# A hybrid decoder block: Conformer merge and part of the output projection as seven-product blocks, with aligned operands

## The chip, the cores and the metric

The kernel runs on one core of one Trainium2 chip. The metric is the device time of one execution in microseconds; the median of several runs is compared. Before the change it is 906.48 us (3 runs, 906.36 to 908.56).

## The reference

One block of a decoder over 512 tokens and 1,024 channels in float32. A norm, one wide projection, three token mixers (dilated attention, a Conformer convolution, a short convolution), a sigmoid gate for each mixer, a merge, an output projection with residual, then a gated MLP with a convolution and a last norm.

```
h = rms_norm(x, norm1_g)
u = h @ w_in
q, k, v, conf_a, conf_gate, sc_b, sc_c, sc_x, gates = split(u)
attn  = dilated_window_attention(...) @ w_attn_out      # 256 -> 1024
conf  = silu(layer_norm(dwconv31(conf_a * sigmoid(conf_gate)))) @ w_conf_out   # 768 -> 1024
short = (sc_b * dwconv3(sc_c * sc_x)) @ w_sc_out         # 768 -> 1024
g = sigmoid(gates)                                       # 3 x 1024 channels
mixed = g[0] * attn + g[1] * conf + g[2] * short
x = x + mixed @ w_o                                      # 1024 -> 1024
up = dwconv3(rms_norm(x, norm2_g) @ w_up)
return rms_norm(x + (silu(f_gate) * f_val) @ w_down, final_g)
```

## The kernel before, in words

Activations are kept transposed: 128 channels on the partitions, 512 tokens along the free axis. A tile is one such 128x512 block in float32. Every operand of a product is split into a high and a low part (names ending in h and l, whi and wlo for weights); a product is hi·hi + hi·lo + lo·hi, three matmuls that add up in one PSUM bank.

**Weights.** The host packs all weights into steps of eight 128x128 units, 128x1024 floats each, in the order in which they are used. For each step SP starts a DMA into one of four buffers (tiles w, r or s), ACT casts the high part (whi, L258), and the low part is either a DVE subtraction (wlo, L263) or, where by_dma says so, ACT writes minus the high part into wlo (L260) and POOL starts a DMA that adds the step's weights to it in SBUF (L261). This preparation runs AHEAD = 3 steps ahead of the matmuls, with four buffers each for whi and wlo.

**Quads.** The gates' projection, and most of w_up, are done as quads (function quad): a 2x2 block of output (two channel groups, two token halves of 256) by seven products instead of eight. The seven weight operands are, in this order, r11, s1, s2, r12, s3, s4, r22. Three of them are loaded quarters of the block. s1 = r21 + r22 is loaded by SP and added to by a POOL DMA, in one of two extra buffers; s2, s3, s4 are made from the others by DVE subtractions of whole steps (L224). The activation operands are b11, b21, b22 (halves of the tiles) and four sums t1 to t4, made by x_sums: for each of the quad's row pairs, four 256-wide subtractions on DVE, two casts of 512 on ACT, two subtractions for the low parts on DVE. A product has K/2 · 2 · 3 matmuls of 256 columns: 24 for K = 8 row blocks. A quad uses the PSUM banks a, b and c. Banks b and c (kinds qb and qc) have one buffer each, so a quad's second product, which opens bank c, waits until the previous quad's bank c has been read.

**Around the change.** The gates for one mixer and four output groups are one quad (gt01 is row half 0 of mixer 1, the Conformer). Its four results go through a sigmoid on ACT (tiles sg, L920). Then merge multiplies the mixer's own output projection (tile mo) by sg and adds it to mixed (tile mx). For the Conformer this is four output tiles of 18 matmuls with 512 columns for each half (K = 6), after which mixed is split into mx..h and mx..l. The order is gt02, gt12, the attention's gt00 and merge, gt10 and merge, gt01, merge, gt11, merge. The output projection follows: eight tiles wo of 24 matmuls with 512 columns, residual and split for the second norm (xh) behind each. w_up follows.

**What sets the order.** Each engine's instructions are put in order at build time by a scheduler that works from the program's order; side work is put in a queue and taken from it at slots, each piece behind an anchor instruction. Engines run in order, so an instruction that waits holds up all that stand behind it on that engine.

Of the kernel before, what the change touches and what calls it, by code (L numbers as in the profile page):

```python
# [53 lines left out]
FW = SW + KC * 3  # L54
NPAR = FW + 2 * KF * 3


# [3 lines left out]

def quad_units(name, pairs):

    return [(name, 2 * i + odd, p[f]) for f, odd in ((0, 0), (0, 1), (1, 0), (1, 1)) for p in pairs for i in range(KD // 2)]


def plan():

    steps = [("n", c) for c in range(54)]
    c = 54  # L70
    for name, _, n in BRANCHES:
        for q in range(2):
# [12 lines left out]

def weight_units():

    aw = CONF // P
    a0, g0 = 18, 18 + aw
    b0, c0, x0 = 30, 36, 42  # L90
    gate0 = 48
    u = []
    for js in ((0, 1), (2,), (3,), (4,), (5,)):
        for k in range(KD):
            u += [("w_in", k, m + j) for j in js for m in (a0, g0)]
    for g in range(3):
        for m in (0, 6):
            for p in range(2):
                u += [("w_in", k, m + 2 * g + p) for k in range(KD)]
        if g < 2:  # L100
            for k in range(KD):
                u += [("w_in", k, (12, 14)[g] + p) for p in range((2, 4)[g])]
    for j in range(KC):
        for m in (c0, x0, b0):
            u += [("w_in", k, m + j) for k in range(KD)]
    u += [("w_sc_out", k, j) for j in range(KD) for k in range(KC)]
    for name, br, n in BRANCHES:
        for q in range(2):
            c = gate0 + br * KD + 4 * q
            u += quad_units("w_in", [(c, c + 1), (c + 2, c + 3)])  # L110
            u += [(name, k, 4 * q + i) for i in range(4) for k in range(n)] if name != "w_sc_out" else []
    for j in range(KD):
        u += [("w_o", k, j) for k in range(KD)]
# [44 lines left out]
def trunk(ctx: ExitStack, tc: tile.TileContext, xT, wts, par, bias, sel, ident, fg, out):  # L158
    nc = tc.nc
    cp = ctx.enter_context(tc.tile_pool(name="cp", bufs=1))  # L160
    wp = ctx.enter_context(tc.tile_pool(name="wp", bufs=3))
    tp = ctx.enter_context(tc.tile_pool(name="tp", bufs=49))
    early = ctx.enter_context(ExitStack())
    ap = ctx.enter_context(tc.tile_pool(name="ap", bufs=KC))
    sp = ctx.enter_context(tc.tile_pool(name="sp", bufs=2))
    kp = ctx.enter_context(tc.tile_pool(name="kp", bufs=8))
    psum = ctx.enter_context(ExitStack())
# [40 lines left out]
    def w_source(c):  # L208
# [8 lines left out]
        def quarter(n):  # L217
            t = w_tile(c, n)
            nc.sync.dma_start(t, wts[i + ("r11", "r12", "r21", "r22").index(n)])
            quarters[i, n] = t  # L220
            return t

        q = lambda n: quarters[i, n]
        sub = lambda o, a, b: V.tensor_tensor(out=o, in0=a, in1=b, op=ALU.subtract)  # L224
        if kind in ("r11", "r12"):
            t = quarter(kind)
        elif kind == "s1":
            t = quarters[i, "s"] = late["s"].tile([P, UNIT * P], F32, tag="s", name=f"s_{c}")
            nc.sync.dma_start(t, wts[i + 2])
            nc.gpsimd.dma_start(t, wts[i + 3], accum_op=ALU.add)  # L230
        elif kind == "s2":
# [24 lines left out]
    def w_split(c, s):  # L256
        hi, lo = (q[:, s] for q in w_parts(c))
        A.copy(hi, w32s[c][:, s])  # L258
        if by_dma(c):
            anchor[0] = A.activation(lo, hi.bitcast(F32), AF.Copy, scale=-1.0).ins  # L260
            nc.gpsimd.dma_start(lo, wts[steps[c][1]], accum_op=ALU.add)  # L261
            return
# [8 lines left out]
    def ahead(c):  # L271

        while state["prepped"] <= min(c + AHEAD, len(steps) - 1):
            p = state["prepped"]
            w_source(p)
            with ExitStack() as order:
                if p == 4:
                    for q in last:
                        order.enter_context(tc.issue_after(q))
                w_split(p, slice(0, UNIT * P))  # L280
            if p + 1 < len(steps):
# [43 lines left out]

    par_sb = cp.tile([P, NPAR], F32, name="par_sb")

# [16 lines left out]
    ident_sb = cp.tile([P, P], F32, name="ident_sb")  # L344
    sel32 = cp.tile([4, 256], F32, name="sel32")
    sel_sb = cp.tile([4, 256], F32R, name="sel_sb")
# [420 lines left out]

    def x_sums(y, k, parts):
# [3 lines left out]
        hi, lo = (kp.tile([P, 4 * HALF], F32R, tag="kb", name=f"xs{k}{n}") for n in "hl")  # L772
        G = V
        for g in range(2):
# [9 lines left out]
            o = slice(g * S, (g + 1) * S)  # L784
            A.copy(hi[:, o], t)
            G.tensor_tensor(out=lo[:, o], in0=t, in1=hi[:, o].bitcast(F32), op=ALU.subtract)
        for i, n in enumerate(("t1", "t2", "t3", "t4")):
            x[n] = tuple(q[:, i * HALF : (i + 1) * HALF] for q in (hi, lo))
        return x

    def hn_sums(k):
        y = []
        for i in range(2):
            t = t512(name=f"hs{k}{i}")
            hi, lo = hn[2 * k + i]
            tt(t, hi.bitcast(F32), lo.bitcast(F32), ALU.add)
            y.append(t)
        xs[k] = x_sums(y, k, hn)

# [7 lines left out]

    def quad(x, name, done, sum22=None):

        beside = slot_ if sum22 is None else lambda _: side(3)  # L810

        def product(bank, n, fresh=False):
# [5 lines left out]
            for p in range(2):  # L818
                o = bank[:, p * HALF : (p + 1) * HALF]
                for k in range(KD // 2):  # L820
                    b = slice((p * 4 + k) * P, (p * 4 + k + 1) * P)
                    xh, xl = x[k][n]
                    T.matmul(o, hi[:, b], xh, start=fresh and p == k == 0, stop=False, skip_group_check=True)
                    T.matmul(o, hi[:, b], xl, start=False, stop=False, skip_group_check=True)
            for p in range(2):
                o = bank[:, p * HALF : (p + 1) * HALF]
                for k in range(KD // 2):
                    b = slice((p * 4 + k) * P, (p * 4 + k + 1) * P)
                    T.matmul(o, lo[:, b], x[k][n][0], start=False, stop=k == KD // 2 - 1, skip_group_check=True)

# [81 lines left out]

    mixed = [None] * KD

    def gates(q, br):
# [9 lines left out]
    def merge(j, br, g):  # L925
# [47 lines left out]
    x1 = []  # L973
    for j in range(KD):
        ps = ps512(f"wo{j}")
        tile_mm(ps, mixed, j == 0)
        tt(xr[j], ps, xr[j], ALU.add)
        x1.append(xr[j])
        xg2.append(split(xr[j], f"xh{j}", pc(G2 + j)))
        q = t512(name=f"s2{j}")  # L980
        A.activation(q, xr[j], AF.Square)
        sq2.append(q)
        if j == 1:
            acc2 = t512(name="acc2")
            tt(acc2, sq2[0], sq2[1], ALU.add)
        elif j > 1:
            tt(acc2, acc2, q, ALU.add)

# [179 lines left out]
    for t in range(4):  # L1168
        pieces = [(0, slice(0, S))] + ([(1, slice(0, S))] if t < 3 else [(1, slice(0, HALF)), (1, slice(HALF, S))])
        sums = []  # L1170
        for n, (h, cols) in enumerate(pieces):
            for k in range(KF - KEEP, KF):
                down(k, t, (h,), cols)
            if n == len(pieces) - 1:
                bm = most(t, sums)
            sums.append(residual(t, h, cols, n))
        finish(t, bm, sums[-1])
# [53 lines left out]
```

## Time and profile before

| | before |
|---|---|
| median of 3 runs | 906.48 us (906.36 to 908.56) |
| the profiled execution | 907.52 us |
| its span, first to last instruction | 905.7 us |
| mean granted TensorE clock | 0.998 |
| PE busy | 894.3 us, 99% |
| weight load (PEld) busy | 795.7 us, 88% |
| DVE busy | 669.4 us, 74% |
| ACT busy | 533.1 us, 59% |
| POOL busy | 92.8 us, 10% |

The profiled execution is some 1 us above the median. Busy time is the time in which an engine has an instruction in work; a matmul's own duration covers its passage through the array, so the matmuls' starts, not their durations, tell how fast PE goes. All times in the views are microseconds from the span's start.

### The profile page before, as it was taken

To read this page: it belongs to the slowest core of one execution; us is meant where nothing else is said; L and a number is where in the kernel's file an instruction comes from. 1 tells how busy PE (TensorE), PEld (TensorE's weight loads), DVE (VectorE), ACT (ScalarE), POOL (GpSimd) and SP (SyncE) were. 2 spreads that over 40 slices of the span, in tenths; PEclk is the share of its full clock that TensorE was granted. 3 is DMA by queue.
4 is the path that set the end of the run, shared out by engine and by line. 5 is a ranking of instruction groups with operands and counts; after the bars stand their busy time and mean duration, and the time that the engine had idled before them with its cause. 6 is when DMAs were issued, how large, how long until landed. Compare 5 with 4: busy or idle time off the path is not lost.

```text
span 905.7 us, 13395 instructions
## 1 busy us (share of the span) xinstructions
PE 894.3 (99%) x5208; PEld 795.7 (88%) x5208; DVE 669.4 (74%) x943; ACT 533.1 (59%) x823; POOL 92.8 (10%) x118
## 2 busy tenths in 40 slices
PE   9999999999999999999999999999999999999996
PEld 7888989888887879999989888889999999888885
DVE  6679969947999868976575545896898889952225
ACT  7655566656656769744544356766766777831214
POOL 3011112211111100000000011100000000000002
PEclk9999999999999999999999999999999999999999
DMA  8688776776797746666636568855666764443202
GB/s 314 191 196 200 181 181 140 167 169 157 181 212 169 161 92 163 189 161 186 187 84 194 188 159 188 190 114 146 179 165 164 182 168 121 154 131 107 93 1 93
DMA packets 42984, 145.32 MB, mean 160 GB/s; under 512 B 4900, under 2 KB 5416, under 8 KB 42920
## 3 DMA queue, kind: packets, MB, share of 16 engines
q1 hardware_dynamic: 30248, 98.84, 32.3%
q0 software_dynamic: 12384, 45.09, 29.9%
q8 instruction: 41, 0.67, 0.3%
q10 hardware_dynamic: 288, 0.52, 0.2%
q14 instruction: 23, 0.19, 0.1%
HBM read 142.34 MB, written 2.10 MB: 159 GB/s over the span
## 4 chain that ended last, share of the span: by engine, by line
PE 91%; ACT 3%; DMA 2%; DVE 2%; issue 1%; SPq 0%; POOL 0%; ACTq 0%; POOLq 0%
PE dn L1121 4%; PE dn L1119 4%; PE dn L1120 4%; PE mo L310 3%; PE mo L311 3%; PE mo L313 3%; PE up L310 2%; PE up L311 2%; PE up L313 2%; DMA wlo<-wts 2%; PE wo L311 1%; PE wo L313 1%; PE wo L310 1%; PE pv L606 1%; PE pv L605 1%; PE pv L604 1%
## 5 line engine op out<-in xcount | busy, mean ns | idle before, releaser
L258 ACT CAST whi<-w 128x1024 fp32r<-128x1024 f32 (+2 forms) x109 | 110.2, 1011 | 161.3 <-PE dn L1120 66.0
L506 DVE SCALAR_TENSOR_TENSOR cc<-ca,par_sb,cc 128x512 f32<-128x512 f32 x180 | 124.2, 743 | 0.2
L263 DVE TENSOR_TENSOR wlo<-w,whi 128x1024 fp32r<-128x1024 f32 (+2 forms) x51 | 57.0, 1117 | 75.3 <-ACT whi L258 74.7
L261 POOL DMA_DIRECT2D wlo<-wts x72 | 62.8, 872 | 431.3 <-ACT wlo L260 351.1
L258 ACT CAST whi<-r 128x1024 fp32r<-128x1024 f32 x70 | 72.9, 1049 | 48.4 <-PE mo L311 10.3
L260 ACT ACTIVATE wlo<-whi 128x1024 fp32r<-128x1024 f32 x72 | 76.3, 1059 | 16.0 <-PE px L313 4.0
L263 DVE TENSOR_TENSOR wlo<-r,whi 128x1024 fp32r<-128x1024 f32 x56 | 68.2, 1219 | 10.5 <-ACT whi L258 7.9
L1033 DVE SCALAR_TENSOR_TENSOR uc<-uu,par_sb,uc 128x511 f32<-128x511 f32 (+1 forms) x72 | 52.0, 746 | 12.4 <-ACT uc L1028 11.9
L263 DVE TENSOR_TENSOR wlo<-s,whi 128x1024 fp32r<-128x1024 f32 x28 | 34.1, 1219 | 9.1 <-ACT whi L258 4.9
L258 ACT CAST whi<-s 128x1024 fp32r<-128x1024 f32 x28 | 29.3, 1046 | 18.2 <-DVE s L224 13.4
L230 POOL DMA_DIRECT2D s<-wts x14 | 12.8, 916 | 223.5 <-DMA s<-wts 53.3
L646 ACT ACTIVATE sc<-sc,nm 128x256 f32<-128x256 f32 (+1 forms) x32 | 15.6, 489 | 17.9 <-DVE nm L644 17.9
L1028 ACT ACTIVATE uc<-uu,par_sb 128x512 f32<-128x512 f32 x36 | 25.2, 728 | 0.3 <-DVE uu L363 0.3
L1119 PE MATMUL dn<-whi,fb 128*128 128x512 f32 x64 | 24.9, 389 | 0.0
L1120 PE MATMUL dn<-whi,fb 128*128 128x512 f32 x64 | 24.9, 389 | 0.0
L1121 PE MATMUL dn<-wlo,fb 128*128 128x512 f32 x64 | 24.9, 389 | 0.0
L1147 POOL TENSOR_TENSOR x1t<-x1t,fg 128x512 f32<-128x512 f32 x4 | 5.6, 1392 | 140.5 <-ACT jk L1129 140.5
L363 DVE TENSOR_TENSOR xr<-wo,xr 128x512 f32<-128x512 f32 x8 | 5.5, 692 | 18.6 <-PE wo L313 16.4
L363 DVE TENSOR_TENSOR sg<-mo,sg 128x512 f32<-128x512 f32 x16 | 11.0, 687 | 10.4 <-PE mo L313 10.2
L224 DVE TENSOR_TENSOR r<-r,r 128x1024 f32<-128x1024 f32 x14 | 17.1, 1224 | 0.4
L224 DVE TENSOR_TENSOR s<-s,r 128x1024 f32<-128x1024 f32 x14 | 17.1, 1222 | 0.3
L224 DVE TENSOR_TENSOR r<-r,s 128x1024 f32<-128x1024 f32 x14 | 17.1, 1218 | 0.0
(3027 smaller groups left out, 3208.7 us busy)
## 6 DMA issues: line engine op xcount, KB each, us to landing
w<-wts SPq DMA_DIRECT2D x100, 512.0 KB, 3.6
wlo<-wts POOLq DMA_DIRECT2D x72, 512.0 KB, 5.8
r<-wts SPq DMA_DIRECT2D x56, 512.0 KB, 4.3
s<-wts SPq DMA_DIRECT2D x14, 512.0 KB, 4.4
s<-wts POOLq DMA_DIRECT2D x14, 512.0 KB, 8.0
xr<-xT SPq DMA_DIRECT2D x8, 256.0 KB, 5.5
xT<-xT SPq DMA_DIRECT2D x7, 256.0 KB, 5.5
w<-wts SPq DMA_DIRECT2D x7, 256.0 KB, 5.5
```

The source lines that it names most:

```text
L258: A.copy(hi, w32s[c][:, s])
L260: anchor[0] = A.activation(lo, hi.bitcast(F32), AF.Copy, scale=-1.0).ins
L261: nc.gpsimd.dma_start(lo, wts[steps[c][1]], accum_op=ALU.add)
L263: anchor[0] = V.tensor_tensor(out=lo, in0=w32s[c][:, s], in1=hi.bitcast(F32), op=ALU.subtract).ins
L310: T.matmul(ps, w[k][0], x[k][0], start=k == 0, stop=False)
L311: T.matmul(ps, w[k][0], x[k][1], start=False, stop=False)
L313: T.matmul(ps, w[k][1], x[k][0], start=False, stop=k == n)
L506: return lambda: V.scalar_tensor_tensor(out=cacc[j], in0=apad[j][:, t : t + 512], scalar=pc(CW + j * CONF_K + t), in1=cacc[j], op0=ALU.mul ...
L1033: V.scalar_tensor_tensor(out=c[:, d:], in0=u[:, : 512 - d], scalar=pc(w + t), in1=c[:, d:], op0=ALU.mult, op1=ALU.add)
L1119: T.matmul(o, fh, wh, start=k == 0, stop=False, skip_group_check=True)
L1120: T.matmul(o, fl, wh, start=False, stop=False, skip_group_check=True)
L1121: T.matmul(o, fh, wl, start=False, stop=k == KF - 1, skip_group_check=True)
```

## The change

The Conformer's merge becomes two quads (merge_quad), one for each half of the output channels, over three pairs of row blocks, K = 6, with weight steps that are 768 wide. Its operand sums are made by conf_sums(k), k = 0 to 2, which are put in the queue when gt01 begins, at a cost of 0.1 each. The output projection does tiles 0 and 1 as before, tiles (2, 3) and (4, 5) as one quad with sums by mx_sums(k), then tiles 6 and 7 as before; tile 0 takes its inputs in the order FIRST. Padding moves all weight and activation tiles to addresses that are multiples of 2,048 bytes (before, nearly all started 96 bytes behind one). The load of s1 is issued two steps earlier in the program. In the tail the last output tile's second half is no longer cut in two, and one multiplication by the final gain goes from POOL to DVE.

```diff
+WO = (0, 1, 6, 7)
+WQ = ((2, 3), (4, 5))
+FIRST = (0, 1, 2, 3, 4, 6, 5, 7)
+PAR_PAD = 608
...
+            if name == "w_conf_out":
+                steps += [(kind, c) for kind in QUAD]
+                NARROW.add(c)
+                c += 4
+                continue
...
+    steps += [("n", c), ("n", c + 1)]
+    steps += [(kind, c + 2) for kind in QUAD]
+    steps += [("n", i) for i in range(c + 6, UP + 2 * PLAIN)]
...
             w_source(p)
+            if steps[p + 3 : p + 4] and steps[p + 3][0] == "s1":
+                w_source(p + 3)
...
-    par_sb = cp.tile([P, NPAR], F32, name="par_sb")
+    par_sb = cp.tile([P, PAR_PAD], F32, name="par_sb")[:, :NPAR]
...
-                for k in range(KD // 2):
-                    b = slice((p * 4 + k) * P, (p * 4 + k + 1) * P)
+                for k in range(len(x)):
+                    b = slice((p * len(x) + k) * P, (p * len(x) + k + 1) * P)
...
+    def mx_sums(k):
+        ms[k] = x_sums(mx32[2 * k : 2 * k + 2], k, mixed)
...
+    def merge_quad(q, g):
+        def done(f, h, src):
+            o = slice(h * HALF, (h + 1) * HALF)
+            for p in range(2):
+                t, m = g[2 * p + f][:, o], mixed[4 * q + 2 * p + f][:, o]
+                tt(t, src[:, p * HALF : (p + 1) * HALF], t, ALU.mult)
+                tt(m, m, t, ALU.add)
+            if f + h == 1:
+                for p in range(2):
+                    j = 4 * q + 2 * p + f
+                    mx32[j] = mixed[j]
+                    mixed[j] = split(mixed[j], f"mx{j}")
+        quad(cq, f"mo{q}", done)
+    def conf_sums(k):
+        cq[k] = sums_of(conf, k, True)
     for name, br, n in BRANCHES:
+        if br == 1:
+            conv.credit = 0.0
+            for k in range(KC // 2):
+                conv.add(lambda k=k: conf_sums(k), 0.1)
         for q in range(2):
             g = gates(q, br)
             slot()
...
+            if br == 1:
+                if q == 1:
+                    for i in range(2):
+                        mx_sums(i)
+                conv.drain()
+                merge_quad(q, g)
+                continue
...
+    for j in WO:
+        ps = ps512(f"wo{j}")
+        tile_mm(ps, [mixed[k] for k in (FIRST if j == 0 else range(KD))], j == 0)
+        if j == 0:
+            for k in range(2, 4):
+                mx_sums(k)
+        tt(xr[j], ps, xr[j], ALU.add)
+        wo_out(j)
+        if j == WO[1]:
...
+            quad(ms, "wo", done, None, lambda _: None)
...
-        nc.gpsimd.tensor_tensor(out=y[0], in0=y[0], in1=fg_sb[0], op=ALU.mult)
...
-        pieces = [(0, slice(0, S))] + ([(1, slice(0, S))] if t < 3 else [(1, slice(0, HALF)), (1, slice(HALF, S))])
+        pieces = [(0, slice(0, S))] + [(1, slice(0, S))]
```

How the change moves instructions is seen best at two engines. First ACT from gt01's copies on (whi are weight casts, sg the sigmoids, which read the banks gt01a, gt01p, gt01c and gt01b; mx0h is the split of mixed). Before:

```order
L841 COPY gt01p_4305<-gt01c_4275 128x512
L258 CAST whi_90_4338<-r22_90_4311 128x1024
L258 CAST whi_91_4370<-w32_91_4342 128x1024
L920 ACTIVATE sg0100_4237<-gt01a_4241 128x256
L920 ACTIVATE sg0110_4239<-gt01a_4241 128x256
L258 CAST whi_92_4403<-w32_92_4374 128x1024
L920 ACTIVATE sg0101_4238<-gt01p_4305 128x256
L920 ACTIVATE sg0111_4240<-gt01p_4305 128x256
L258 CAST whi_93_4435<-w32_93_4407 128x1024
L920 ACTIVATE sg0100_4237<-gt01c_4275 128x256
L920 ACTIVATE sg0110_4239<-gt01c_4275 128x256
```

Now, from the casts of the second operand sums (xs) on:

```order
L818 CAST xs10h_4329<-xt10_4333 128x512
L818 CAST xs11h_4330<-xt11_4338 128x512
L285 CAST whi_93_4490<-s_92_4361 128x768
L285 CAST whi_94_4523<-r12_94_4494 128x768
L818 CAST xs20h_4347<-xt20_4351 128x512
L818 CAST xs21h_4348<-xt21_4356 128x512
L961 ACTIVATE sg0100_4237<-gt01a_4241 128x256
L961 ACTIVATE sg0110_4239<-gt01a_4241 128x256
L961 ACTIVATE sg0101_4238<-gt01p_4305 128x256
L961 ACTIVATE sg0111_4240<-gt01p_4305 128x256
L961 ACTIVATE sg0100_4237<-gt01c_4275 128x256
L961 ACTIVATE sg0110_4239<-gt01c_4275 128x256
```

All eight sigmoids of gt01 stood between weight casts, each pair soon after its bank was done; now they stand in one row behind the last of the six casts xs00h to xs21h.

DVE in the same place of the changed kernel (hs is a tile put together from its parts, xt the sums, L250 a weight subtraction, L290 a weight's low part); all of these rows stand behind gt01c, and behind gt01p:

```order
L817 TENSOR_TENSOR xt11_4338<-hs11_4327,xt10_4333 128x256
L250 TENSOR_TENSOR s_92_4361<-s_92_4361,r11_91_4399 128x768
L819 TENSOR_TENSOR xs11l_4332<-xt11_4338,xs11h_4330 128x512
L392 TENSOR_TENSOR hs20_4343<-cf4h_3438,cf4l_3439 128x512
L392 TENSOR_TENSOR hs21_4345<-cf5h_3518,cf5l_3519 128x512
L812 TENSOR_TENSOR xt20_4351<-hs20_4343 128x256
L290 TENSOR_TENSOR wlo_93_4491<-s_92_4361,whi_93_4490 128x768
L813 TENSOR_TENSOR xt20_4351<-hs21_4345,xt20_4351 128x256
L290 TENSOR_TENSOR wlo_94_4524<-r12_94_4494,whi_94_4523 128x768
L819 TENSOR_TENSOR xs20l_4349<-xt20_4351,xs20h_4347 128x512
L816 TENSOR_TENSOR xt21_4356<-hs21_4345,hs20_4343 128x256
L817 TENSOR_TENSOR xt21_4356<-hs21_4345,xt20_4351 128x256
```

Before, between gt01c and the first merge multiplication DVE had four low parts of weights and gt01p; now these rows of the sums stand there too, and xs21h of ACT's row waits for the second xt21.

DVE at the seam from the Conformer's second quad to the output projection (mx5l and mx7l are inputs of wo0, xs2l and xs3l operand sums of the wo quad, s_115 its s1):

```order
L392 TENSOR_TENSOR mx7_3148<-mx7_3148,sg1111_4734 128x256
L384 TENSOR_TENSOR mx5l_5189<-mx5_3089,mx5h_5188 128x512
L290 TENSOR_TENSOR wlo_115_5214<-s_115_5093,whi_115_5213 128x1024
L384 TENSOR_TENSOR mx7l_5193<-mx7_3148,mx7h_5192 128x512
L250 TENSOR_TENSOR s_115_5093<-s_115_5093,r11_114_5129 128x1024
L250 TENSOR_TENSOR r11_114_5129<-r11_114_5129,r21_118_5317 128x1024
L392 TENSOR_TENSOR xr0_5196<-wo0_5212,xr0_5196 128x512
L290 TENSOR_TENSOR wlo_116_5275<-s_115_5093,whi_116_5274 128x1024
L392 TENSOR_TENSOR xr1_5198<-wo1_5273,xr1_5198 128x512
L812 TENSOR_TENSOR xt20_5244<-mx4_3053 128x256
L816 TENSOR_TENSOR xt21_5249<-mx5_3089,mx4_3053 128x256
L813 TENSOR_TENSOR xt20_5244<-mx5_3089,xt20_5244 128x256
```

Before, mixed was split tile by tile and each wo tile was followed by one low part of weights, one split and one sum of squares. Now a low part of 1,024 stands between mx5l and mx7l, and twelve rows of sums stand behind xr1, which waits for the tile wo1.

## Rows read from the trace of the kernel before

**Rows 1.** The page, part 1: busy time of each engine.
```profile
PE 894.3 (99%) x5208; PEld 795.7 (88%) x5208; DVE 669.4 (74%) x943; ACT 533.1 (59%) x823; POOL 92.8 (10%) x118
```

**Rows 2.** Busy time, granted clock and DMA by stretch (us), for all engines.
```profile
400.00:510.00 110.00, 110.00 (x724) 101.44 (x723) 71.81 (x84) 48.43 (x74) 4.33 (x5) 1.00 0.54 156
510.00:555.00 45.00, 45.00 (x200) 37.19 (x200) 20.58 (x28) 24.75 (x31) 4.10 (x5) 1.00 0.65 175
```

**Rows 3.** PE's waits over the whole span: total us, times, longest.
```profile
PE gt00a L829 <- DMA wlo<-wts: 0.5, 1, 0.5
```

**Rows 4.** The chain of waits, 425 to 560 us: start, us, what.
```profile
432.10 0.96 PE gt01a L829 x8
...
434.98 0.96 PE gt01c L829 x8
...
453.09 1.36 PE mo L313 x6
...
457.17 1.36 PE mo L313 x6
...
512.26 1.81 PE wo L313 x8
517.70 1.81 PE wo L313 x8
```

**Rows 5.** PE in order of time: first matmul of gt01, first of the Conformer's merge.
```profile
430.03 0.28 PE L823 MATMUL gt01a<-hn0h,whi 128*128 128x256 f32 x1
...
450.18 0.40 PE L310 MATMUL mo<-cf0h,whi 128*128 128x512 f32 x1
```

**Rows 6.** DVE in order of time, 307 to 309 us: operand sums of the gate quads.
```profile
307.10 0.69 DVE L363 TENSOR_TENSOR hs<-hn4h,hn4l 128x512 f32<-128x512 f32 x1
307.70 0.68 DVE L363 TENSOR_TENSOR hs<-hn5h,hn5l 128x512 f32<-128x512 f32 x1
308.31 0.42 DVE L778 TENSOR_TENSOR xt<-hs 128x256 f32<-128x256 f32 x1
308.64 0.42 DVE L782 TENSOR_TENSOR xt<-hs,hs 128x256 f32<-128x256 f32 x1
```

**Rows 7.** DVE in order of time, 432 to 452 us: the last gate quad of row half 0.
```profile
433.05 1.22 DVE L224 TENSOR_TENSOR r<-r,s 128x1024 f32<-128x1024 f32 x1
434.19 1.22 DVE L263 TENSOR_TENSOR wlo<-r,whi 128x1024 fp32r<-128x1024 f32 x1
...
438.93 0.70 DVE L363 TENSOR_TENSOR gt01c<-gt01b,gt01p 128x512 f32<-128x512 f32 x1 [1.60 <-PE gt01b L829]
```

**Rows 8.** ACT in order of time, the same stretch.
```profile
441.78 0.65 ACT L920 ACTIVATE sg<-gt01a 128x256 f32<-128x256 f32 x2
...
447.54 0.65 ACT L920 ACTIVATE sg<-gt01c 128x256 f32<-128x256 f32 x2
```

**Rows 9.** Groups of instructions, shapes apart: the casts of operand sums on ACT.
```profile
L785 ACT CAST xs0h<-xt 128x512 fp32r<-128x512 f32 x4 | 2.4, 609 | 0.9 <-DVE xt L779 0.7
```

**Rows 10.** The page, part 6: DMA issues, KB each, median us to landing.
```profile
wlo<-wts POOLq DMA_DIRECT2D x72, 512.0 KB, 5.8
```

**Rows 11.** The chain of waits at gt00a's late DMA: start, us, what.
```profile
369.87 0.85 POOL s L230
...
371.77 8.79 DMA wlo<-wts
```

**Rows 12.** PE and DVE in order of time, the last microseconds.
```profile
896.88 0.28 PE L1121 MATMUL dn<-wlo,fh21h 128*128 128x256 f32 x1
897.96 0.39 PE L1119 MATMUL dn<-whi,fh19h 128*128 128x256 f32 x1 [0.80 <-DVE fb L1138]
...
899.32 0.42 DVE L363 TENSOR_TENSOR x1t<-dn,x1t 128x256 f32<-128x256 f32 x1
```

**Rows 13.** Clock and busy time by stretch, after the last matmul; warm-up matmuls.
```profile
903.00:905.00 2.00, 0.00 (x0) 0.00 (x0) 0.00 (x0) 0.00 (x0) 0.00 (x0) 0.50 0.55 208
...
1.20 3.78 PE L320 MATMUL warm<-zero 128*128 128x256 f32 x16 [1.20 <-DVE zero L317]
```

More of the change, by code (lines that the diff above doesn't have):

```diff
@@ L55, with quad_units @@
 NPAR = FW + 2 * KF * 3
+PAR_PAD = 608
 BRANCHES = (("w_sc_out", 2, KC), ("w_attn_out", 0, 2), ("w_conf_out", 1, KC))
-def quad_units(name, pairs):
-    return [(name, 2 * i + odd, p[f]) for f, odd in ((0, 0), (0, 1), (1, 0), (1, 1)) for p in pairs for i in range(KD // 2)]
+def quad_units(name, pairs, n=KD):
+    return [(name, 2 * i + odd, p[f]) for f, odd in ((0, 0), (0, 1), (1, 0), (1, 1)) for p in pairs for i in range(n // 2)]
+NARROW = set()
 def plan():
@@ L110, in weight_units @@
             u += quad_units("w_in", [(c, c + 1), (c + 2, c + 3)])
-            u += [(name, k, 4 * q + i) for i in range(4) for k in range(n)] if name != "w_sc_out" else []
-    for j in range(KD):
-        u += [("w_o", k, j) for k in range(KD)]
+            if name == "w_attn_out":
+                u += [(name, k, 4 * q + i) for i in range(4) for k in range(n)]
+            elif name == "w_conf_out":
+                c = quad_units(name, [(4 * q, 4 * q + 1), (4 * q + 2, 4 * q + 3)], n)
+                for i in range(0, len(c), n):
+                    u += c[i : i + n] + [c[i]] * (UNIT - n)
+    for j in WO:
+        u += [("w_o", k, j) for k in (FIRST if j == 0 else range(KD))]
+        if j == WO[1]:
+            u += quad_units("w_o", [tuple(q) for q in WQ])
     for j in range(PLAIN):
@@ L162, in trunk @@
     tp = ctx.enter_context(tc.tile_pool(name="tp", bufs=49))
+    kp = ctx.enter_context(tc.tile_pool(name="kp", bufs=8))
     early = ctx.enter_context(ExitStack())
@@ L196, in trunk, with width @@
     anchor = [None]
+    def width(c):
+        kind, i = steps[c]
+        return (KC if i in NARROW else KD) * P
     def w_tile(c, name):
@@ L218, in quarter @@
             t = w_tile(c, n)
[L219 removed]
+            nc.sync.dma_start(t[:, :w], wts[i + ("r11", "r12", "r21", "r22").index(n)][:, :w])
             quarters[i, n] = t
@@ L260, in w_split @@
             anchor[0] = A.activation(lo, hi.bitcast(F32), AF.Copy, scale=-1.0).ins
-            nc.gpsimd.dma_start(lo, wts[steps[c][1]], accum_op=ALU.add)
+            nc.gpsimd.dma_start(lo, wts[steps[c][1]][:, s], accum_op=ALU.add)
             return
@@ L344, in trunk @@
     ident_sb = cp.tile([P, P], F32, name="ident_sb")
-    sel32 = cp.tile([4, 256], F32, name="sel32")
+    sel32 = t512(name="sel32")[0:4, :256]
     sel_sb = cp.tile([4, 256], F32R, name="sel_sb")
@@ L766, in trunk, with x_sums @@
     HALF = S // 2
-    def x_sums(y, k, parts):
+    def x_sums(y, k, parts, apart=False):
         x = {n: tuple(q[:, h * HALF : (h + 1) * HALF] for q in parts[2 * k + i]) for n, i, h in (("b11", 0, 0), ("b21", 1, 0), ("b22", 1, 1))}
         b11, b12, b21, b22 = (y[i][:, h * HALF : (h + 1) * HALF] for i in range(2) for h in range(2))
-        hi, lo = (kp.tile([P, 4 * HALF], F32R, tag="kb", name=f"xs{k}{n}") for n in "hl")
+        if apart:
+            his = [ap.tile([P, S + CONF_K - 1], F32R, tag="ap", name=f"xs{k}{g}h")[:, :S] for g in range(2)]
+            los = [t512(F32R, f"xs{k}{g}l") for g in range(2)]
+        else:
+            hi, lo = (kp.tile([P, 4 * HALF], F32R, tag="kb", name=f"xs{k}{n}") for n in "hl")
+            his, los = ([q[:, g * S : (g + 1) * S] for g in range(2)] for q in (hi, lo))
         G = V
@@ L806, in side, with quad @@
             n -= 1
-    def quad(x, name, done, sum22=None):
-        beside = slot_ if sum22 is None else lambda _: side(3)
+    def quad(x, name, done, sum22=None, beside=None):
+        beside = beside or (slot_ if sum22 is None else lambda _: side(3))
         def product(bank, n, fresh=False):
@@ L826, in product @@
                 o = bank[:, p * HALF : (p + 1) * HALF]
-                for k in range(KD // 2):
-                    b = slice((p * 4 + k) * P, (p * 4 + k + 1) * P)
-                    T.matmul(o, lo[:, b], x[k][n][0], start=False, stop=k == KD // 2 - 1, skip_group_check=True)
+                for k in range(len(x)):
+                    b = slice((p * len(x) + k) * P, (p * len(x) + k + 1) * P)
+                    T.matmul(o, lo[:, b], x[k][n][0], start=False, stop=k == len(x) - 1, skip_group_check=True)
         a = ps512(name + "a")
@@ L973, in trunk, with wo_out, done @@
     x1 = []
[L974 to L979, printed above, removed]
+    def wo_out(j):
+        x1.append((j, xr[j]))
+        xg2.append((j, split(xr[j], f"xh{j}", pc(G2 + j))))
         q = t512(name=f"s2{j}")
         A.activation(q, xr[j], AF.Square)
[L982 to L987, printed above, removed]
+        if not sq2:
+            sq2.append(q)
+        else:
+            tt(sq2[0], sq2[0], q, ALU.add)
+    for j in WO:
+        ps = ps512(f"wo{j}")
[5 more added lines that the diff above has]
+        wo_out(j)
+        if j == WO[1]:
+            def done(f, h, src):
+                for p in range(2):
+                    t, o = WQ[p][f], slice(h * HALF, (h + 1) * HALF)
+                    tt(xr[t][:, o], src[:, p * HALF : (p + 1) * HALF], xr[t][:, o], ALU.add)
+                if f + h == 1:
+                    for p in range(2):
+                        wo_out(WQ[p][f])
+            quad(ms, "wo", done, None, lambda _: None)
+    x1 = [t for _, t in sorted(x1, key=lambda q: q[0])]
+    xg2 = [t for _, t in sorted(xg2, key=lambda q: q[0])]
+    acc2 = sq2[0]
     h2 = [None] * KD
```

34 lines of the change are left out of this document (20 added, 14 removed).

## The prediction

> **What bounds the kernel now.** I read the page's busy times first: PE is busy 894.3 of 905.7 us, every other engine has room [rows 1]. So a change pays only by giving PE less to stream, and costs what it makes PE wait. The busy times by stretch say the same of the place of the change: from 400 to 555 us PE is busy throughout at a granted clock of 1.00, while DVE is idle for (110.00 − 71.81) + (45.00 − 20.58) = 62.6 us and ACT for 81.8 us [rows 2]. PE's waits are few; the one to see is the gate quad gt00, which waited 0.5 us for a wlo that a DMA had to complete [rows 3]. The chain of waits runs through PE there, and its starts give the rates [rows 4]: a quad product of 24 matmuls with 256 columns takes 434.98 − 432.10 = 2.88 us, 0.120 each; a Conformer tile of 18 matmuls with 512 columns 4.08 us and an output tile of 24 takes 5.44 us, 0.2267 each.
>
> **What PE saves.** One Conformer half is 4 · 4.08 = 16.32 us; as a quad it is 7 products of 18 matmuls, 126 · 0.120 = 15.12. That is −1.2, twice. Four output tiles are 21.76 us; the quad is 168 · 0.120 = 20.16, −1.6. Together −4.0 us. It is not an eighth, since a matmul of half the columns costs more than half: 0.120 against 0.113. The rates fit a fixed part of 13.3 ns for each matmul on top of its columns at 2.4 GHz (0.2133 and 0.1067), and the quads issue more matmuls.
>
> The Trainium skill ("TensorE: Matmul & The Clock Gate", section Back-to-back issue gap) puts that fixed part at about 2.5 ns. By it the three quads would save 1.78 + 1.78 + 2.37 = 5.9 us, an estimate from its formula. The rows show 13.3 ns, and I stay with them.
>
> **What hides under PE.** The operand sums, narrower low parts and the merge in halves give DVE about 49 us of new work at the durations of their kinds: 0.42 for 256 columns, 0.69 for 512 [rows 6], 1.22 for 1,024 [rows 7], 0.95 between them for 768. ACT gets about 23 us. I cost this work at nothing where the idle time covers it. But 49 of DVE's 62.6 is close, so the order decides, at four places.
>
> **First place: the second product of the Conformer's first quad, mo0.** It opens bank c. That bank has one buffer, last held by gt01c, whose sigmoids must have read it. Before, ACT did those at 447.54, between weight casts [rows 8]. In the new order they stand behind the casts of all six operand sums; the last, xs21h, waits for DVE's second xt21. DVE's chain to it can be added up. It starts with gt01c at 438.93, which waits for PE as before [rows 7]. From there to xt21 DVE has, by its order, 11 rows of 512, 10 of 256, 4 of 768 and 1 of 1,024. Their pitches are 0.60 for 512 (307.10 to 307.70), 0.335 for 256 (308.31 to 308.64) [rows 6], and 1.14 for 1,024 (433.05 to 434.19) [rows 7]; 0.87 lies between for 768. That is 6.60 + 3.35 + 3.48 + 1.14 = 14.57 us, so 453.5. I add 1.1 for two casts of 0.61 [rows 9] that DVE itself waits for: 454.6. Then the cast of xs21h 0.61, and the three sigmoid pairs of gt01a, gt01p and gt01c, 0.65 each [rows 8]: 457.15. PE wants the bank at 430.03, gt01's first matmul [rows 5], plus 7 · 2.88 for gt01 and 18 · 0.120 for mo0's first product: 452.35. **PE waits 4.8 us.** With no wait inside DVE it is 3.7, with twice the waits 5.9. The sums themselves are late too: xs20l, two rows before the end of that chain, comes about a microsecond after mo0's second product wants it, so the sigmoids alone are not all of it.
>
> **Second: the DMA-added low parts.** The r11 steps of gt11 and mo1 get their wlo by ACT and a POOL DMA. The three steps in front of gt11 were 5.44 each, and are 2.16 as narrow products. So from the start of the preparation to the first use (16 hi matmuls into gt11) there are 3 · 2.16 + 1.92 = 8.4 us, for two ACT passes (2.0) and the landing, 5.8 in the median [rows 10] and 8.79 behind another POOL DMA at gt00 [rows 11]: between 0.6 early and 2.4 late. I take 0.4, since the DMA in front is some microseconds older here. For mo1's r11, ACT stands behind the sigmoids of gt11a and POOL behind the s of the same quad; issued about 4.4 us ahead of the quad, landing 6.7 later, needed 1.44 into it: 0.9 (0 to 2).
>
> **Third: the first output tile.** At the end of mo1 the last results of mixed are multiplied, added, cast and split. A low part of 1,024 (1.14) stands between mx5l and mx7l on DVE. From the quad's end: four 256-wide rows beside two splits 2.6, mx5l 0.6 behind its cast 0.6, 1.14, mx7l 0.6, hops 0.5: 6.0. FIRST puts mx5 and mx7 last, mx7 22 matmuls or 5.0 into the tile. I take 1.0 (0 to 1.6).
>
> **Fourth: the wo quad.** DVE makes its sums for mixed 4 to 7 behind xr1, which waits for tile wo1. The quad's second product wants xs3l 2.88 + 0.84 after wo1's end. DVE has xr1, eight 256-wide rows, xs2l twice and then xs3l, about 5.3 with the casts: 1.6 late (0.5 to 2.5).
>
> **The tail.** The cut of the last tile cost PE a wait of 0.80 [rows 12]; without it the last matmul starts about 1.0 earlier. The last residual is 512 wide (+0.27), so is its square (+0.2), and the multiplication by the gain stands before it on DVE (+0.6): +0.1 in all (−0.7 to 0.5).
>
> **Loads.** The earlier s1 moves nothing in the quads of w_up: SP's and POOL's orders are unchanged there, and POOL still has its s ahead of the next wlo. Cost and gain nothing. The few POOL DMAs more lie in POOL's idle time, 90% of the span [rows 1]. What alignment does to DMA, DVE and ACT the trace can't tell; I take nothing.
>
> **The sum.** −4.0 + 4.8 + 0.4 + 0.9 + 1.0 + 1.6 + 0.1 = +4.8 us. The profiled execution took 907.52, so it would take 912.3. It was 1.0 above the median of 906.48; against that the forecast is **911.3**, and with the ends of the terms about 908.5 to 914. A measurement of this kernel can tell about 0.3%, 2.7 us, from no change: faster means below 903.8, slower above 909.2.
>
> **Rivals.**
> - *The small waits hide.* Only the first place costs its full price; the 4.8 us pause gives the later preparations time. −4.0 + 4.8 + 0.1 = +0.9: 907.4, no change. For it: PE now stands still, while DVE, ACT and the DMAs go on. Against: the second to fourth place come 13 us and more behind, with work of their own. 0.27.
> - *The casts are ready.* On the other side: if ACT reaches gt01c's sigmoids by 450.4, PE doesn't wait at mo0 and the later places shrink to little: −4.0, 902.5, **faster**. That needs DVE at xt21 by 449.8, with 10.9 us for rows that cost 14.57 at the traced pitch. It decides from three quarters of that pitch on; nothing in the rows goes so fast. 0.11.
> - *Alignment takes the fixed part away.* Nearly all operands start at 96 bytes past a multiple of 2,048, and all full-clock matmuls show the 13.3 ns. If the start address causes it, 5,208 matmuls [rows 1] give back up to 69 us: about 837. For it: the warm-up on `zero`, which starts at a multiple of 128, took 3.78 us for 16 [rows 13], about the bare column time at 1.2 GHz plus one pause. Against: this is at the other clock level, and halves that cross a 2,048-byte line cost the same as those that don't. 0.07.
> - *The clock falls in the pause.* The granted clock was 0.50, the 1.2 GHz level, at 903 to 905, when PE had been without a matmul since 899.3 [rows 13]. At that level a 256-column matmul takes about twice 0.107 instead of 0.120, so a stretch as long as the warm-up's 3.78 us loses 1.7 us, twice if a second pause does the same: 913 to 915. For it: 4.8 us is longer than any pause in this trace. Against: it was 1.00 through the waits of 0.5 and 0.8 us [rows 3, 12], and those were short. 0.10.
> - *The change doesn't do what it says for s1*, as worked out; it moves no term.
>
> The Trainium skill's 2.5 ns in the section named above would make the alignment rival 10.8 ns for each of the 5,208 matmuls, 56 us, about 850; no row here shows an aligned operand at the 2.4 GHz level.
>
> **How the numbers follow.** The forecast case has 0.45, and a little of its range lies within 2.7 us. Faster: 0.11 + 0.07 and some of the first rival's lower end, 0.20. Same: 0.28. Slower: 0.52. The range reaches from 902.0, which takes in the case without waits, to 915.5, with the fallen clock; the alignment case is left out.
>
> **What would show it.** Right: PE's waits name mo0c waiting for ACT's sg by 4 to 6 us; mo1a and gt11a for DMA wlo; wo for mx7l and xs3l; quad products of 2.16 us for K = 6, and 0.120 between matmuls as before. Wrong: no PE wait at mo0c, a matmul pitch below 0.115, or a granted clock below 1.00 behind the pause.

## The result, and the profile after

The changed kernel takes 920.27 us (median of 4 runs, 913.40 to 921.25) against 906.47: the ratio is 1.0128, 95% interval 1.0096 to 1.0161, so it is slower, by 1.3%. The profiled execution took 921.1 us, with a span of 919.3 and a mean granted clock of 0.990. One of the four runs took 913.4, at a mean clock of 0.996; the other three 919.4 to 921.3, all at 0.990.

The page's busy times, which answer to [rows 1]:

```profile
PE 899.4 (98%) x5379; PEld 807.4 (88%) x5379; DVE 709.4 (77%) x1034; ACT 552.7 (60%) x854; POOL 95.9 (10%) x122
```

PE is 5 us busier and its span is 13.6 us longer. The waits of PE, which answer to [rows 3], name the places:

```profile
PE mo0c L859 <- ACT sg L961: 4.8, 1, 4.8
PE wo L326 <- ACT mx4h L383: 1.9, 1, 1.9
PE mo1a L865 <- DMA wlo<-wts: 1.8, 1, 1.8
...
PE woc L859 <- ACT xs3h L818: 0.7, 1, 0.7
PE woc L860 <- DVE xs3l L819: 0.5, 1, 0.5
PE wo L327 <- DVE mx4l L384: 0.2, 1, 0.2
```

Stretches of the changed kernel with busy time of PE, PEld, DVE, ACT and POOL, granted clock, DMA share and GB/s, which answer to [rows 2, 13]:

```profile
453.00:458.00 5.00, 0.75 (x7) 0.55 (x5) 5.00 (x9) 2.48 (x7) 0.00 (x0) 0.98 0.02 4
458.00:462.00 4.00, 3.47 (x16) 3.47 (x17) 1.40 (x2) 2.74 (x7) 0.00 (x0) 0.50 0.75 236
462.00:466.00 4.00, 4.00 (x26) 4.00 (x26) 1.10 (x2) 1.75 (x3) 0.86 (x1) 0.68 0.77 169
498.00:502.00 4.00, 4.00 (x24) 4.00 (x23) 1.77 (x3) 0.57 (x1) 0.00 (x0) 0.59 0.46 167
510.00:515.00 5.00, 5.00 (x36) 4.63 (x35) 4.61 (x12) 1.26 (x2) 0.00 (x0) 1.00 1.02 379
515.00:520.00 5.00, 2.91 (x10) 1.59 (x9) 2.43 (x5) 4.09 (x6) 0.86 (x1) 0.92 1.04 405
520.00:523.00 3.00, 3.00 (x10) 2.34 (x9) 3.00 (x4) 0.19 (x1) 0.00 (x0) 0.57 1.09 257
```

In the first of these stretches PE does almost nothing for five microseconds, and DVE is busy all the time. Then PE works, but at a granted clock of 0.50, the 1.2 GHz level: 16 matmuls in the 3.5 us of 458.5 to 462, where at 0.120 there would be 29, and 26 in the next 4 us where there would be 33. The same returns behind 498 and behind 520. Before, the clock read 1.00 in this part of the program [rows 2].

ACT in the changed kernel in order of time, which answers to [rows 8]:

```profile
456.14 0.62 ACT L818 CAST xs21h<-xt 128x512 fp32r<-128x512 f32 x1 [1.52 <-DVE xt L817]
456.67 0.65 ACT L961 ACTIVATE sg<-gt01a 128x256 f32<-128x256 f32 x2
457.21 0.72 ACT L961 ACTIVATE sg<-gt01p 128x256 f32<-128x256 f32 x2
457.82 0.66 ACT L961 ACTIVATE sg<-gt01c 128x256 f32<-128x256 f32 x2
```

and DVE at the same place, [rows 7] before:

```profile
453.54 0.43 DVE L813 TENSOR_TENSOR xt<-hs,xt 128x256 f32<-128x256 f32 x1
...
455.34 0.43 DVE L816 TENSOR_TENSOR xt<-hs,hs 128x256 f32<-128x256 f32 x1
455.68 0.43 DVE L817 TENSOR_TENSOR xt<-hs,xt 128x256 f32<-128x256 f32 x1
```

The three sigmoid pairs stand behind xs21h, xs21h behind DVE's second xt, and PE starts mo0's second product at 458.53, when the pair of gt01c is through.

The chain of waits at the other two places, and two quad products (start, us, what):

```profile
467.19 0.72 PE mo0a L865 x6
469.33 0.72 PE mo0b L865 x6
...
488.97 0.48 POOL s L257
489.49 8.13 DMA wlo<-wts
...
505.54 8.30 DMA r<-wts
513.94 1.07 ACT whi L285
...
517.02 0.53 ACT mx4h L383
```

For mo1, POOL's own s stands just ahead of the wlo, which takes 8.13 us. At the output projection the load of the quad's r11 step takes 8.30 us, beside three more r loads that SP starts behind it and, in its last 2 us, the first of the residual's; the DMA share is 1.02 from 510 to 515. ACT waits for it (the first of the two whi rows), and the cast of mx4 stands behind ACT's two passes over that step and the cast of the next one, s1 (515.99). The rows of mo0a and of the next mo0b start 2.14 us apart: 18 matmuls at about 0.120. The aligned operands go at the pitch of before [rows 4].

**Where the 13.6 us went.** I add up, for consecutive matmuls, what their starts lie apart beyond the pitch of 0.2267 or 0.120. From 400 to 560 us that is 0.1 us before and 17.3 now. Of these 5.0 come from matmuls at the lower clock level (2.4, 1.4 and 1.2 behind the three pauses) and 12.3 from waits. The rows above name 9.9 of that; the rest are wider gaps between the starts around the same waits (5.2 us at mo0c against the 4.8 named, 3.1 at wo0 against 2.1), which no view names. At the start there are 1.5 us more, since in this execution PE's matmuls came at half pace until 10.4 us, and before until 6.0. The rest of the program gives back 2.0, of which about 1.0 is the cut tile's wait at the end [rows 12]. What PE has to stream is 4.2 us less. From the last matmul's start to the end it is 7.83 us instead of 6.74, 1.1 more. 17.2 + 1.5 − 2.0 − 4.2 + 1.1 = 13.6.

### The profile page after: what moved, and what is told of

It is laid out like the page before. It is cut to its first block, busy times and chain, and to the rows that moved or that the text cites. A ratio compares the mean times of both kernels' runs of the same rounds, so it can differ in the third digit from the quotient of the medians.

```text
span 919.3 us, 13919 instructions
## 1 busy us (share of the span) xinstructions
PE 899.4 (98%) x5379; PEld 807.4 (88%) x5379; DVE 709.4 (77%) x1034; ACT 552.7 (60%) x854; POOL 95.9 (10%) x122
## 4 chain that ended last, share of the span: by engine, by line
PE 85%; DVE 5%; DMA 5%; ACT 2%; issue 2%; POOL 0%; ACTq 0%; POOLq 0%; DVEq 0%
PE dn L1211 4%; PE dn L1213 4%; PE dn L1212 4%; DMA wlo<-wts 3%; PE up L339 2%; PE up L340 2%; PE up L342 2%; PE mo L339 1%; PE mo L340 1%; PE mo L342 1%; DVE wlo L290 1%; PE pa L327 1%; PE pa L326 1%; PE pv L635 1%; PE pv L634 1%
## 5 line engine op out<-in xcount | busy, mean ns | idle before, releaser
L285 ACT CAST whi<-r 128x1024 fp32r<-128x1024 f32 (+1 forms) x85 | 86.2, 1026 | 57.6 <-DVE r L250 7.8
L290 DVE TENSOR_TENSOR wlo<-w,whi 128x1024 fp32r<-128x1024 f32 (+2 forms) x42 | 46.1, 1097 | 70.9 <-ACT whi L285 70.9
L290 DVE TENSOR_TENSOR wlo<-r,whi 128x1024 fp32r<-128x1024 f32 (+1 forms) x68 | 80.5, 1190 | 15.9 <-ACT whi L285 11.7
L290 DVE TENSOR_TENSOR wlo<-s,whi 128x1024 fp32r<-128x1024 f32 (+1 forms) x34 | 40.4, 1189 | 9.2 <-ACT whi L285 5.0
L285 ACT CAST whi<-s 128x1024 fp32r<-128x1024 f32 (+1 forms) x34 | 34.7, 1021 | 21.2 <-DVE s L250 13.7
L250 DVE TENSOR_TENSOR r<-r,r 128x1024 f32<-128x1024 f32 (+1 forms) x17 | 20.3, 1194 | 0.4
L250 DVE TENSOR_TENSOR s<-s,r 128x1024 f32<-128x1024 f32 (+1 forms) x17 | 20.3, 1191 | 0.3
L250 DVE TENSOR_TENSOR r<-r,s 128x1024 f32<-128x1024 f32 (+1 forms) x17 | 20.2, 1191 | 0.0
L392 DVE TENSOR_TENSOR mx<-mx,sg 128x512 f32<-128x512 f32 (+1 forms) x32 | 16.9, 554 | 0.1
L392 DVE TENSOR_TENSOR ptl<-pt,pth 128x512 fp32r<-128x512 f32 (+1 forms) x16 | 10.5, 655 | 5.6 <-ACT pth L686 5.3
```

The source lines that it names most:

```text
L250: sub = lambda o, a, b: V.tensor_tensor(out=o[:, :w], in0=a[:, :w], in1=b[:, :w], op=ALU.subtract)
L290: anchor[0] = V.tensor_tensor(out=lo, in0=w32s[c][:, s], in1=hi.bitcast(F32), op=ALU.subtract).ins
```

## The experiments

All times are medians, beside runs of the kernel before on the same chip (906.85 for the first four, 907.24 for the next three, 907.31 and then 906.94 for the last ones). Theory A is the prediction's, with the clock: the saved stream is real, waits at the three quads take it back, and the clock falls behind the longest. Its rivals were a cost of the small parts or of alignment, of the output quad, or of DVE's work as such.

### The small parts alone

The kernel before, with the padding, the s1 load and the tail:

```diff
+PAR_PAD = 608
+            if steps[p + 3 : p + 4] and steps[p + 3][0] == "s1":
+                w_source(p + 3)
-        nc.gpsimd.tensor_tensor(out=y[0], in0=y[0], in1=fg_sb[0], op=ALU.mult)
+                eng = V if t == 3 else nc.gpsimd
```

> The kernel before with the padding to multiples of 2,048 bytes, the s1 load two steps earlier and the new tail; no new quad. Theory A (the loss is PE's waits around the three new quads, and the clock's fall behind them): these parts are worth nothing but the tail's wait of about 1 us, which other work takes up: 905.5 to 907, matmul pitch still 0.227 and 0.120. Theory B (one of these parts costs something all over the program): 909 or more. Theory C (the aligned operands pay by a shorter matmul pitch): under 900.

Measured: 906.29 us, ratio 1.000 (0.9991 to 1.001). The matmul pitch is unchanged, so theories B and C fall. In the tail PE's wait is gone, and the time from the last matmul's start to the end grew by 1.0: no gain. As to s1: with its two lines left out of the changed kernel, every engine has the same instructions in the same order as with them, so they change nothing in the program, and there is no run of them alone.

### Each quad alone

The output projection as eight plain tiles again, the Conformer's quads kept:

```diff
-    steps += [("n", c), ("n", c + 1)]
-    steps += [(kind, c + 2) for kind in QUAD]
...
-            quad(ms, "wo", done, None, lambda _: None)
```

> The changed kernel with the output projection as eight plain tiles again. Theory A: two quads save 2.4 us of stream; the waits at mo0c (about 5) and mo1a (about 1.9) stay, and the clock falls behind them (2.4 and 1.4); no wait at woc, and none of 2.9 at wo0, since no r11 step is loaded there: 911 to 915. Rival (the output projection's quad is what costs): 904 to 907.

Measured: 916.04 us, ratio 1.010 (1.0085 to 1.0115), a microsecond over the expected range. PE's waits, and its clock by stretch:

```profile
PE mo0c L855 <- ACT sg L957: 4.8, 1, 4.8
PE mo1a L861 <- DMA wlo<-wts: 3.3, 1, 3.3
```

```profile
458.00:462.00 4.00, 3.90 (x18) 3.90 (x19) 0.98 (x2) 2.63 (x6) 0.00 (x0) 0.50 0.87 221
...
494.00:498.00 4.00, 0.75 (x7) 0.54 (x6) 1.21 (x2) 0.83 (x1) 0.00 (x0) 1.00 1.00 308
498.00:502.00 4.00, 4.00 (x34) 4.00 (x35) 1.76 (x2) 1.89 (x3) 0.86 (x1) 1.00 0.33 104
```

The wait at mo0c is the same 4.8, and the clock fell behind it. mo1a waited 3.3 instead of 1.8, but no fall followed there.

The Conformer's merge as plain tiles again, the output projection's quad kept:

```diff
-            if name == "w_conf_out":
-                steps += [(kind, c) for kind in QUAD]
...
-                merge_quad(q, g)
-                continue
```

> The changed kernel with the Conformer's merge as eight plain tiles again (18 matmuls of 512 columns each). Theory A: the quad saves 1.6 us of stream; waits of 1 to 2 at woc for xs3, up to 2 at wo0; no wait at gt01's end, the clock holds or falls once: 905 to 909. Rival: 911 or more.

Measured: 904.64 us, ratio 0.9974 (0.9965 to 0.9984): **faster than before** by its interval, though by less than 0.3%, and at the quad PE waits for nothing, neither at wo0 nor at woc. That is a little better than expected (905 to 909, with waits at both). So the output quad's waits in the changed kernel came from what stands ahead of it.

### The pause filled

38 matmuls on the tile of zeros between mo0's first and second product, their result not used:

```diff
+        if name == "mo0":
+            fill = ps512("fill")
+            for _ in range(38):
+                T.matmul(fill[:, :WIDE], zero[:, :P], zero, start=True, stop=True)
```

> The changed kernel with 38 more matmuls of 256 columns on the tile of zeros, into a bank of their own, between mo0's first and second product; their result is not used. Theory A (the pause there makes the granted clock fall, and that costs 2.4 us on top of the pause): the fill takes 38 x 0.120 = 4.56 us of the 4.9 us pause, the clock stays at 1.00 from 453 to 466, and the profile is 2 to 3 us shorter than that of the change with its fall. Rival (the clock falls for another reason): the same stretch at 0.50 to 0.68 again, time as the change or longer.

Measured: 913.46 us (911.53 to 913.86), ratio 1.0067 (1.0052 to 1.0082). PE in order of time, and the stretches as above:

```profile
452.35 4.72 PE L877 MATMUL fill<-zero 128*128 128x256 f32 x38
```

```profile
453.00:458.00 5.00, 4.78 (x40) 4.57 (x40) 4.20 (x7) 3.48 (x11) 0.00 (x0) 1.00 0.24 77
458.00:462.00 4.00, 4.00 (x36) 4.00 (x35) 1.94 (x3) 3.12 (x5) 0.46 (x1) 1.00 0.73 230
462.00:466.00 4.00, 4.00 (x35) 4.00 (x35) 2.96 (x6) 2.64 (x4) 0.41 (x1) 1.00 0.80 192
```

The clock stays at 1.00 with nothing else mended: a fall costs extra, and the first one came from PE standing still. The profile is 7.3 us shorter than the change's, not 2 to 3. The starts of the other matmuls tell why: the two later falls are missing as well (2.6), the start was 1.6 quicker, and the waits at wo0 are about 1.9 us shorter, with r11's load at 6.58 us instead of 8.30, against a new wait of 1.0 at gt11. What is left, 913.5, is a kernel with most of the waits and at full clock. That the later falls went away because the first pause was filled is not shown: other things moved too. The fill's matmuls, on a tile at a multiple of 128 bytes, go 0.120 apart like all others.

### The sums a quad earlier

```diff
-        if br == 1:
-            conv.credit = 0.0
-            for k in range(KC // 2):
-                conv.add(lambda k=k: conf_sums(k), 0.1)
         for q in range(2):
+            if br == 0 and q == 1:
+                conv.credit = 0.0
+                for k in range(KC // 2):
+                    conv.add(lambda k=k: conf_sums(k), 0.7)
```

> The changed kernel with conf_sums put in the queue one gate quad earlier, at gt10, one per slot; nothing else moved. Theory A (gt01c's sigmoids are late because they stand on ACT behind casts that wait for DVE's sums): no wait at mo0c, clock 1.00 throughout, the wait at mo1a of 1 to 2 stays, woc 1.6 stays; against the kernel with the filled pause (913.5) 4 to 5 us less: 907 to 910. Rival (DVE is simply too full, the sums delay something else by as much): 912 or more, with a new wait of PE between 404 and 450.

Measured: 920.14 us, ratio 1.0131 (1.0104 to 1.0157). PE's waits, and the chain at the new place:

```profile
PE mo0a L865 <- DMA wlo<-wts: 5.4, 1, 5.4
```

```profile
438.86 0.68 DVE xs21l L819
...
440.60 1.23 DVE r L250
...
441.84 4.57 DMA s<-wts
...
447.00 0.49 POOL s L257
...
447.51 10.71 DMA wlo<-wts
```

The wait at mo0c is gone, so it did hang on those sums. But the rival's time (912 or more) was right, though its new wait came at 452.5 and not before 450: the sums, now in the attention's merge, push DVE's weight work for gt01 back (r at 440.60, behind xs21l), with it SP's reload of an s buffer, and POOL takes mo0's wlo only behind that s: it lands at 458.2, 5.4 us late. A new wait, within a microsecond of the same time, of about the same size. The clock, expected at 1.00, fell behind it and again behind mo1a's wait of 2.4, and not behind wo0's of 1.7.

### The r11 low parts by DVE

```diff
-        return kind == "r11"
+        return kind == "r11" and not min(NARROW) < i < UP
```

> The changed kernel with the low parts of the r11 steps of gt11, mo1 and the output projection's quad made by DVE, not by ACT and a POOL DMA. Theory A: mo1a's wait for the DMA (1.9) goes, wo0's wait for mx4h shrinks by the ACT pass that stood ahead of it (1.0); mo0c's pause and the clock's fall behind it stay: 2 to 4 us under the change, 915.5 to 918.5 where the clock falls. Rival (DVE has no room there): the waits come back as waits for DVE's low parts, 920 or more.

Measured: 911.30 us (910.82 to 913.07), ratio 1.0051 (1.0035 to 1.0066), 9 us under the change where 2 to 4 were expected. PE's waits:

```profile
PE mo0c L859 <- ACT sg L961: 4.8, 1, 4.8
...
PE wob L859 <- DVE woc L392: 0.6, 1, 0.6
```

The waits at mo1a and at wo0 are gone, the second wholly: r11's load was there after 5.3 us instead of 8.30, ACT had one pass over it instead of two, and the cast of mx4 was in time. Which of these decided isn't shown. mo0c's pause stays. The clock fell behind it (1.4 us) and, with no later pause, not again: from 400 to 560 us PE's starts lie 8.2 us beyond the pitch instead of 17.3.

### All together

Both edits, and the output quad behind three plain tiles:

```diff
+LAST = 2
-        if j == WO[1]:
+        if j == WO[LAST]:
```

> Both of these edits together, and the output projection's quad one plain tile later (tiles 0, 1, 6, quad, 7). Theory A (the saved stream of 4.0 us is real, and only waits and the clock hid it): no wait over 0.5 us at mo0c, mo1a and woc; 902 to 904.5, faster than the kernel before. Rival (each quad brings a wait somewhere that its 1.2 or 1.6 us can't pay for): 906 or more.

Measured: 911.08 us, ratio 1.0041 (1.0028 to 1.0054), where 902 to 904.5 was expected: the rival's range. One long wait was left:

```profile
PE mo0a L866 <- DMA wlo<-wts: 3.7, 1, 3.7
...
PE up14a L866 <- DMA wlo<-wts: 0.4, 1, 0.4
```

It is the one that the earlier sums had made, since mo0's own r11 still went by POOL (the edit's < leaves it out). With it by DVE too:

```diff
-        return kind == "r11" and not min(NARROW) < i < UP
+        return kind == "r11" and not min(NARROW) <= i < UP
```

> The kernel with all three mends (sums early, r11 low parts by DVE, output quad later), with the low part of mo0's own r11 step by DVE as well; the kernel before it waited 3.9 us there for the POOL DMA, and the clock fell (1.1). Theory A (waits and the clock are all that hides the 4.0 us of stream): no wait over 0.5 us between 400 and 555 us, clock 1.00 there; 5 us under that kernel's profile, 902 to 905. Rival (another wait takes its place once more, since the sums keep DVE from the weights): 908 or more.

Measured: 904.56 us (904.11 to 905.07), ratio 0.9972 (0.996 to 0.9984). PE's waits behind the warm-up, and its stretches:

```profile
PE gt02a L860 <- ACT mx L974: 1.1, 1, 1.1
PE up14a L866 <- DMA wlo<-wts: 0.5, 1, 0.5
PE n2ps L1090 <- ACT n2sh L384: 0.4, 1, 0.4
PE gt00a L866 <- DMA wlo<-wts: 0.3, 1, 0.3
PE n2ps L1091 <- DVE n2sl L385: 0.2, 1, 0.2
```

```profile
400.00:450.00 50.00, 50.00 (x380) 48.30 (x379) 47.02 (x65) 26.44 (x43) 2.59 (x3) 1.00 0.51 131
450.00:500.00 50.00, 49.95 (x418) 49.75 (x417) 46.19 (x73) 28.32 (x45) 2.61 (x3) 1.00 0.58 168
500.00:555.00 55.00, 54.39 (x321) 48.01 (x320) 45.87 (x73) 36.09 (x48) 3.46 (x4) 1.00 0.73 215
```

The view names no wait from 400 us to the second norm's sums (n2ps, 0.6 in all), and the clock is at 1.00. DVE is busy 93 of 100 us from 400 to 500, and that is enough, as long as its order is right. The same with plain output tiles:

> The same mends (sums early, r11 low parts of gt11 and both Conformer quads by DVE), with the output projection as eight plain tiles. Theory A (each quad is worth its own 1.2 us once nothing waits): about 1.6 us slower than the kernel with the output quad too, 904 to 906. Rival (the Conformer's quads can't pay): 908 or more, with waits at mo0 or mo1.

Measured: 905.25 us, ratio 0.9977 (0.9968 to 0.9986), within the expected range, though only 0.7 slower than with the output quad and not 1.6: the two Conformer quads pay too once nothing waits for them. And with the output quad where the change has it:

> As the kernel in which nothing waits any more (sums early, all three r11 low parts by DVE), but with the output projection's quad where the change has it, behind two plain tiles. Theory A (its place moves a wait of about 1 us from the second norm's sums to the quad's own products, no more): 903.5 to 905.5, PE waits at wob or woc of about 1 and none at n2ps. Rival (the quad has to come later, or its sums are late by 1.6 again): 906 or more.

Measured: 904.49 us (11 runs, 904.0 to 910.04), ratio 0.998 (0.9966 to 0.9993). Where 0.6 was lost at n2ps, there is now a wait of 0.8 at wob:

```profile
PE wob L859 <- DVE woc L392: 0.6, 1, 0.6
...
PE wob L859 <- ACT wob L873: 0.2, 1, 0.2
```

So four kernels beat the change, and the kernel before by 0.2 to 0.3%: the output quad alone (904.64), the Conformer's quads alone with the mends (905.25), and both kinds of quads with the mends (904.56 and 904.49). The last two stream 2.4 us less than the first. At n2ps or wob they lose 1.1 and 1.4 of it again, counted from start to start; the profiled spans differ by 1.0 and 0.8 (903.3 against 902.3 and 902.5), the medians by 0.1 and on different chips, and that rest I didn't settle.

## Why the prediction was wrong

It forecast slower, 911.3 with a range up to 915.5, and the time was 920.3. Of the 8.8 us by which the profiled difference (13.6) exceeds the forecast one (4.8), 5.0 are the clock's falls, 3.6 are waits (12.3 from start to start, where the four places had 8.7 in the sum), 1.5 the slower start, and small gains elsewhere take back 1.3. Point by point:

- **The stream, −4.0:** right. Counted between starts it is −4.2; the rest comes from the last tile, which is no longer cut, and from the last matmul, which has no start behind it. The pitches of 0.120 and 0.227 stayed with aligned operands. The alignment rival is refuted, by the small parts alone and by every trace.
- **The first place, 4.8 us at mo0c:** right, 4.8 measured, by the mechanism named: from gt01c to the second xt21 DVE took 15.9 us (15.7 worked out). That chain ended at 456.1 and gt01c's sigmoid pair at 458.5, 1.3 us later than worked out, and PE came 1.2 later too, as gt01c itself did (440.19, not 438.93). Earlier sums take the wait away (and bring another).
- **The second, 0.4 + 0.9:** gt11 didn't wait, mo1a waited 1.8: a size that was off, within its bounds.
- **The third, 1.0 for mx7l:** the wrong instruction, and the worst sized of the waits. PE waited 2.1 for mx4 (3.1 from start to start), whose cast ACT did behind two passes over the output quad's r11, whose load took 8.30. I had looked for DVE rows ahead of the last input, and not for the DMA that ACT's row in front would wait for. With r11 by DVE the wait is gone.
- **The fourth, 1.6 at woc:** 1.2 (0.7 + 0.5) by the view and 1.8 from start to start, as worked out.
- **The tail, +0.1:** right, 1.0 gained ahead of the last matmul and 1.1 lost behind it. **s1, nothing:** right.
- **The clock:** the step that failed. I kept it out of the sum, gave it a chance of 0.10 and priced it at 1.7, or twice that. It fell at three places and cost 5.0 us in the profiled execution; a clock below 1.00 behind the pause was one of the prediction's own signs of being wrong. Three of four runs have that execution's mean clock of 0.990; the one at 0.996, where it fell less, took 913.4, and the filled pause, at 0.998, gives 913.5. So at full clock the kernel lies about 2 us over the forecast, inside the range; from there to 920 it is the clock, with the wait at wo0 that was 1.9 shorter there and 1.6 at the start. My reason against it was that waits of 0.5 and 0.8 us had done nothing [rows 3, 12]. The longest wait behind the warm-up in the trace of before was another, at the first gate quad:

```profile
PE gt02a L823 <- ACT mx L932: 1.2, 1, 1.2
```

The clock read 1.00 through that too. Nothing in that trace told what a pause of two to five microseconds does, so a chance of 0.10 had little under it.

- **The rivals:** "the small waits hide" was wrong, they came at three places beside the first.
- **The sums:** the ends of the terms, added straight, give 906.0 to 917.4, not 908.5 to 914; the narrower figure had no working. The new work was put too high, which touches no term: DVE is 40 us busier (49 was put) and ACT 20 (23).

What stays open is when the clock falls. It fell behind the pauses at mo1a (1.8) and wo0 (2.1) in this execution, and behind 2.4 at mo1a with the sums early, but not behind 3.3 at mo1a in the kernel with the Conformer's quads alone, nor behind 1.7 at wo0 with the sums early: the length of the pause alone doesn't decide it.

## What to carry to other kernels

When a matmul is moved into a bank with one buffer, write down the whole row of the engine that frees the bank, and what each instruction in that row waits for: here eight sigmoids that had run between weight casts were late because six casts of later work stood ahead of them. Price a pause of PE of several microseconds with a fall of the clock behind it, not by its length alone, and mend the longest pause first: here, with it filled, the later falls were gone as well. And when work is moved earlier on a full engine, ask which loads its displaced instructions release: here the wait came back at the same place as a wait for a DMA.

## What the runs showed of the hardware

- A pause of PE of 4.9 us was followed by 5.5 us at the 1.2 GHz level (0.50), which cost 2.4; one of 3.7, in the kernel with all mends but the last, by 2.6 us (1.1). With the pause of 4.9 filled by matmuls on zeros the clock read 1.00 from there to the end of the matmuls.
- Neither operands at multiples of 2,048 bytes nor a tile at a multiple of 128 changed the matmul's pitch at full clock: 0.120 for 256 columns and 0.227 for 512 in all twelve kernels.

The Trainium skill ("TensorE: Matmul & The Clock Gate", section Back-to-back issue gap) gives 262 and 518 cycles for these, 0.109 and 0.216 us, as the gap of isolated matmuls at the 2.4 GHz level. No run here has them as the pitch of a stream of these float32 operands, aligned or not, and the measurement decides.
